# A hybrid trunk layer on one core: a written order that runs over both ends of the Strassen stage, layer norm in three steps, gate stores on SyncE

## The chip, the cores and the metric

The kernel runs on one core of one Trainium2 chip. The metric is the time of one execution on the device, in microseconds (us). A run's profile comes from one profiled execution; its span is the time from the first to the last instruction in the trace, and the execution's own time is a little longer.

The core's engines, as the profile names them: PE (TensorE, matmuls), PEld (its weight loads, which overlap PE), DVE (VectorE), ACT (ScalarE), POOL (GpSimd, here almost only an issuer of DMAs) and SP (SyncE, a queue of DMAs, "SPq" in the profile). Each engine works through its own list of instructions in order and waits on semaphores.

## The reference, cut to what matters

One layer, one batch, 1024 positions, 1024 channels, all in float32:

```python
h = rms_norm(x, g_mix)
z = h @ w_in + b_in                              # 1024 -> 7168 columns
va, ga, xb, gb, sa, sb = split(z, [1024, 1024, 1536, 1536, 1024, 1024])
u = causal_depthwise_conv(va * sigmoid(ga), conv_a_w, conv_a_b)     # width 31
y_a = silu(layer_norm(u, ln_g, ln_b)) @ w_a_out
v = causal_depthwise_conv(xb, conv_b_w, conv_b_b)                   # width 4
v = rg_lru(v, ...)                               # gates by 16 heads, linear recurrence
y_b = (v * gelu(gb)) @ w_b_out
m = sigmoid(sa) * y_a + sigmoid(sb) * y_b
x = x + m @ w_o
x = x + square(relu(rms_norm(x, g_mlp) @ w_1)) @ w_2
return rms_norm(x, g_final)
```

rg_lru computes a gate `a` and an input `b` for every position and channel and then the recurrence h[t] = a[t] h[t-1] + b[t].

## The kernel before, in words

Every matrix product is done in three matmuls: both operands are split into a high part (rounded to the format that TensorE reads at full rate) and a low part (the rest), and high x high, high x low and low x high are summed. A split is made in one of two ways. `split` (L51, L52): ACT copies the high part, DVE subtracts it from the source. `split_dma` (L65 to L67): ACT writes the negated high part into the low tile, a DMA issued by POOL adds the source to it in place (an accumulating DMA), and ACT copies the high part.

Activations are kept transposed: channels on the 128 partitions, positions along the row, in two halves of 512 (`HALVES`). A matmul is 128x128 by 128x512.

The stages, with their place in the profiled span:

- **Stage 1** (to about 369 us): the columns xb, va and ga of the in-projection, in 28 chunks of 128 columns (L686, 48 matmuls each). Beside it run, on ACT and DVE, the width-4 convolution (L437), the head gates (L485 to L493), the scans of the recurrence (`scan_tile`, L526 to L529, one for each of 12 tiles of channels; each result is stored to the DRAM tile `hd` on SP at L530), the product va * sigmoid(ga) (`u_out`, L540 and the DVE operation listed under L413), and the taps of the width-31 convolution (L579 to L595; each finished tile y0 to y7 is stored to `yd` and added to `ysum` at L602).
- **The z stage** (about 378 to 678 us): the columns gb, sa and sb. They are taken in 14 pairs of chunks; each pair is one 2x2 block product done by Strassen's scheme with 7 products (`z_mm`, L822, 12 matmuls each). So there are 98 steps, in the order `zseq`. For a product p, `z_sums` makes the weight sums on DVE, `z_lhs` splits the left operand (tile `zo`) by `split_dma`, `z_post` carries bank results from one product to the next, and `z_out` (L834 to L845) applies gelu or sigmoid. For gb the result is multiplied with the scan's tile, loaded back from `hd` by `z_h` (L853, tile `hb`), and stored to the DRAM tile `hgd`; for sa and sb it is stored to `gates`. Both stores are issued by POOL (L838, L845). The weights come by `z_load` (L779, tile `zw`) on SP. The right operand's sums (`xs` tiles) are made by `x_load`, `x_sum` (L630 and an accumulating DMA) and `x_parts`, from s = 22 of stage 1 (`XS`) into the z stage (`ZX`).
- **The out-projection b** (about 675 to 831 us): `hgd` is loaded as 12 tiles hg0 to hg11, each split, and eight tiles yb0 to yb7 are computed (L91, 72 matmuls each), each multiplied with a gate tile sb into m (L1008).
- **The layer norm** of the convolution's output runs beside yb: the mean `mu` by a matmul with a matrix of equal entries (L968), the eight tiles yn loaded and centred (L973), squared on ACT (L974) and summed on DVE (L976) into `vs`, the variance `var` by a second matmul (L980), the inverse root by `newton_rstd` (L96 to L104), then scaling (L985) and silu (L986). Then the tiles are split into suh and sul, and **ya0 to ya7** follow (L91, about 838 to 928 us).
- The o projection, the MLP up and down and the last norm take the rest, to 1649.7 us.

What sets the order: in stage 1 and the z stage the order is written out by hand (`tc.manual_schedule`), once for stage 1 and once for the z stage. Three clocks `clk` ("P", "A", "V" for PE, ACT and DVE) are advanced by planned costs (`at`), DVE's operations are put off by `later(ready, cost, f, ...)` and placed by `vector_work` in the order of their ready times; `fill(until)` puts convolution taps into DVE's free time as long as the next, at a planned 0.74 us, ends before `until`. After the z stage a scheduler orders the instructions, and the tile pools, whose tiles are reused in turn, set when a load can start: `T` (the large pool), `E` (a small pool of 7), and the z stage's own pools of 8 weight tiles, 4 sums and 7 evacuation tiles. The first tiles of the out-projection (`first_wb`, and the loop over hg0 to hg11) are given a high priority. A scan's step in the written order:

```python
if d == 0:
    scan_exp(g)
    scan_in(3 * g, 3 * g + 1)
elif d == 1:
    scan_in(3 * g + 2)
    scan_root(g)
else:
    for t in [3 * g + d - 2] if s < NC1 - 1 else range(3 * g + d - 2, 3 * g + 3):
        later(rooted[t], 4.8, scan_tile, t)
```

Here `s` is the chunk, `g` a group of three scans and `d` how many chunks have passed since the group's gates were ready.

Of the kernel before, what the change touches and what calls it, by code (L numbers as in the profile page):

```python
# [15 lines left out]
P = 128  # L16
# [14 lines left out]
def trunk_kernel(ctx: ExitStack, tc: tile.TileContext, x, xt_in, vecs, w_in, w_a_out, w_b_out,  # L31
# [358 lines left out]
    taps = {"wait": [], "now": None, "next": None, "left": 0}  # L390

    def fill(until):
        while clk["V"] + 0.74 <= until:
            if taps["now"] is None:
                if taps["next"] is None:
                    if not taps["wait"]:
                        return
                    taps["next"] = conv(taps["wait"].pop(0))
                    next(taps["next"])
                taps["now"], taps["next"], taps["left"] = taps["next"], None, 48  # L400
            if next(taps["now"], None) is None:
# [115 lines left out]
            nc.scalar.activation(r, r, AF.Sqrt)  # L517
            rooted[t] = at("A", 1.06)

    def scan_in(*ts):  # L520
        for t in ts:
            later(0, 1.27, nc.vector.tensor_tensor, gate[1, t], gate[1, t], vt.pop(t), ALU.mult)

    def scan_tile(t):
        a, r, i = at_.pop(t), gate.pop((0, t)), gate.pop((1, t))
# [27 lines left out]
    def conv(j):  # L553
        u = ut.pop(j)
        acc, tmp = T(f"y{j}"), T(f"yt{j}")
        xe, xo = (u[:, h] for h in HALVES)
        p0, p2 = (acc[:, h] for h in HALVES)
        xs, p1 = (tmp[:, h] for h in HALVES)
        bias = cab_c[:, j:j + 1]

        def tap(d):
            w = WA - 1 - d
            return caw[:, w * 8 + j:w * 8 + j + 1]

# [10 lines left out]
        def step(cost=0.74):  # L575
            at("V", cost)
            return True

        nc.vector.tensor_tensor(xs, xe, xo, add)  # L579
        yield step()  # L580
        nc.vector.tensor_scalar(p2, xs, tapsum(0), cab2[:, j:j + 1], ALU.mult, add)
        clk["V"] = max(clk["V"], begun)
        yield step(0.45)
        for k in range(1, NE):
            for o, a, c in ((p0, xe, tap(2 * k)), (p2, xs, tapsum(k)),
                            (p1, xo, tap(2 * k + 1) if k < NE - 1 else None)):
                if c is not None:
                    nc.vector.scalar_tensor_tensor(o[:, k:], a[:, 0:HS - k], c, o[:, k:],  # L588
                                                   ALU.mult, add)
                    yield step()  # L590
        nc.vector.tensor_tensor(p2, p2, p0, sub)
        yield step()
        nc.vector.tensor_tensor(p2, p2, p1, sub)
        yield step()
        nc.vector.tensor_tensor(p0[:, 1:], p0[:, 1:], p1[:, 0:HS - 1], add)  # L595
        nc.sync.dma_start(yd[j], acc)
        yield step()
        if j == 0:
            ysum.append(T("ysum"))
# [77 lines left out]
    def chunk_mm(s, n0, n1):  # L677
# [5 lines left out]
        for n in range(n0, n1):  # L683
# [9 lines left out]
    head_at = {s: n for n, s in enumerate(HS0)}  # L693

    EXP = {head_slot: g for g, head_slot in enumerate(HS0[4 * g + 3] + 1 for g in range(4))}
    XS = {22: ((x_load, 0),), 23: ((x_sum, 0, 11, 12),), 24: ((x_sum, 0, 22),),
          25: ((x_sum, 0, 21), (x_load, 1)), 26: ((x_parts, 0, 6, 7), (x_sum, 1, 11, 12)),
          27: ((x_sum, 1, 22), (x_parts, 0, 5, 4))}
    w_load(3)
    w_load(4)  # L700
    w_parts(3)
    with tc.manual_schedule(engines=ENGINES):
        for s in range(3, NC1):
# [32 lines left out]
            for d in range(5):  # L736
                if s - d in EXP:
                    g = EXP[s - d]
                    if d == 0:
                        scan_exp(g)  # L740
                        scan_in(3 * g, 3 * g + 1)
                    elif d == 1:
                        scan_in(3 * g + 2)
                        scan_root(g)
                    else:
                        for t in [3 * g + d - 2] if s < NC1 - 1 else range(3 * g + d - 2, 3 * g + 3):
                            later(rooted[t], 4.8, scan_tile, t)
            for f, *a in XS.get(s, ()):
                f(*a)
# [34 lines left out]
    def z_sums(i, p):  # L784

        def S_(n, a, b, op_):
            zs[i, n] = t = sp_.tile([P, HS], F32, tag="s", name=f"zs{n}_{i}").rearrange(
                "p (k c) -> p k c", c=P)
            later(0, 0.74, nc.vector.tensor_tensor, t, a, b, op_)

        if p == 7:
            S_(3, z_blk(i, 0, 0), z_blk(i, 1, 0), ALU.subtract)
        elif p == 6:
            S_(1, z_blk(i, 1, 0), z_blk(i, 1, 1), ALU.add)
            S_(2, zs[i, 1], z_blk(i, 0, 0), ALU.subtract)
        elif p == 5:
            S_(4, z_blk(i, 0, 1), zs[i, 2], ALU.subtract)

    def z_lhs(i, p):
        src = z_blk(i, *{1: (0, 0), 2: (0, 1), 4: (1, 1)}[p]) if p in (1, 2, 4) else \  # L800
            zs[i, {3: 4, 5: 1, 6: 2, 7: 3}[p]]
        o = wp.tile([P, 2, 4, P], F32R, tag="w", name=f"zo{i}_{p}")
        split_dma(src, o[:, 0], o[:, 1])
        at("A", 1.24)
        zo[i, p] = o

    def z_bank(i, b):
# [19 lines left out]
    def z_out(i, m_, hf, src, name):  # L827
# [3 lines left out]
        if ci < SA:  # L831
            t = ci - GB
            h = hb.pop((t, hf))
            nc.scalar.activation(a, src, AF.Gelu_apprx_tanh, bias=bias)  # L834

            def mult():
                nc.vector.tensor_tensor(h, h, a, ALU.mult)
                nc.gpsimd.dma_start(hgd[t, :, HALVES[hf]], h)  # L838

            later(at("A", 0.62), 0.74, mult)  # L840
# [14 lines left out]
    def z_post(i, p):  # L855
# [11 lines left out]
        elif p == 5:  # L867
            zb[i, "c"] = c = EV(f"zc22_{i}")
            nc.scalar.activation(c, zb[i, "e"], AF.Copy)
            later(at("A", 0.62), 0.74, nc.vector.tensor_tensor, c, c, zb[i, "f"], ALU.add)  # L870
        elif p == 3:
            z_out(i, 0, 1, zb[i, "e"], None)
        elif p == 4:
            c = zb[i, "u"]
            later(0, 0.74, nc.vector.tensor_tensor, c, c, zb[i, "f"], ALU.add)

    def z_post2(i, p):

# [8 lines left out]
    for i in range(2, NZ):  # L887
        zseq += [(i, 1), (i, 7), (i - 1, 3), (i, 6), (i, 2), (i - 1, 4), (i, 5)]
    zseq += [(NZ - 1, 3), (NZ - 1, 4)]
    ZX = {0: ((x_sum, 1, 21), (x_parts, 1, 6)), 1: ((x_parts, 1, 7),), 3: ((x_parts, 1, 5),),  # L890
          6: ((x_parts, 1, 4),)}
    H_AT = {2: (0, 0), 5: (1, 1), 3: (0, 1), 4: (1, 0)}
    loaded = 0
# [9 lines left out]
        return f(*zseq[n]) if 0 <= n < len(zseq) else None  # L903

    with tc.manual_schedule(engines=ENGINES):
        z_load_to(4)
        for n in range(4):
            z_get(n, z_sums)
# [30 lines left out]
    def E(name, dt=F32, shape=(P, S)):  # L939
        return ep.tile(list(shape), dt, tag="e", name=name)  # L940

    hg = []

    def first_wb():
        ws = []
        for n in range(2):
            raw = T(f"wb0_{n}")
            nc.sync.dma_start(raw[:, 0:6 * P].rearrange("p (k c) -> p k c", c=P), w_b_out[0, n])
            h = T(f"wb0h_{n}", F32R)
            l = T(f"wb0l_{n}", F32R)  # L950
            split(raw[:, 0:6 * P], h[:, 0:6 * P], l[:, 0:6 * P])
            ws += [(h[:, k * P:k * P + P], l[:, k * P:k * P + P]) for k in range(6)]
        return ws

    with tc.high_priority():
        wb0 = first_wb()
        for t in range(12):
            raw = T(f"hg{t}")
            nc.sync.dma_start(raw, hgd[t])
            h, l = (X1 if t == 0 else E if t < 2 else T)(f"hgh{t}", F32R), \  # L960
                (X1 if t == 0 else E if t < 3 else T)(f"hgl{t}", F32R)
            split(raw, h, l)
            hg.append((h, l))

    def layer_norm_steps():
        pm = PS("mu", "ps2")
        for hs in HALVES:
            nc.tensor.matmul(pm[:, hs], onesm, ysum[0][:, hs], start=True, stop=True)  # L968
        vs, sq = E("vs"), E("sq")
        for j in range(8):  # L970
            ya.append(T(f"yn{j}"))
            nc.sync.dma_start(ya[j], yd[j])
            nc.vector.tensor_tensor(ya[j], ya[j], pm, ALU.subtract)  # L973
            nc.scalar.activation(sq if j else vs, ya[j], AF.Square)  # L974
            if j:
                nc.vector.tensor_tensor(vs, vs, sq, ALU.add)  # L976
        yield
        pv = PS("var", "ps2")
        for hs in HALVES:
# [21 lines left out]
    for j in range(8):  # L1001
# [677 lines left out]
```

## Time and profile before

| | us |
| --- | --- |
| median of 3 runs | 1652.23 (1651.26 to 1656.23) |
| the profiled execution's own time | 1651.43 |
| its span | 1649.7 |
| PE busy | 1581.7 (96%) |
| DVE busy | 1096.1 (66%) |
| ACT busy | 875.5 (53%) |
| POOL busy | 235.5 (14%) |

The mean granted clock of TensorE was 0.984 of full speed. The DMA queues moved 308.58 MB. How to read the views: the rows of busy tenths cut the span into 40 slices and give the busy share of each in tenths; the views of waits name an engine, the line that waited, and whose event ended the wait; a timeline lists single instructions with start and duration, and in brackets the idle time before them; the windows give busy times and, at the end, the granted clock, the DMA share and the rate in GB/s. E means the end of the z stage's last product where the text says so.

### The profile page before, as it was taken

Reading aid. Unit: us, or ns where it says so; the run is one execution under the profiler, and the core shown is the slowest. Engines: PE = TensorE matmul, PEld = TensorE weight load, DVE = VectorE, ACT = ScalarE, POOL = GpSimd, SP = SyncE. Lnnn points to the kernel's source line nnn. Section 1 sums busy time; section 2 is a strip of 40 time slices with the busy share of each in tenths; the row PEclk is TensorE's granted clock in tenths of the full one; section 3 lists DMA queues with packets and bytes.
Section 4 is the critical chain, followed back from the end, with each engine's and each line's share of the span. In section 5 each row is a group of like instructions: output and inputs, shape, how many; then the busy total and the mean of one; then the engine's idle time right before and its main releaser. Section 6 shows DMA issues by size and latency. Waiting matters only on the chain.

```text
span 1649.7 us, 18943 instructions
## 1 busy us (share of the span) xinstructions
PE 1581.7 (96%) x6910; PEld 1289.5 (78%) x6910; DVE 1096.1 (66%) x1456; ACT 875.5 (53%) x1168; POOL 235.5 (14%) x306
## 2 busy tenths in 40 slices
PE   8999999995999999799989999999999999999998
PEld 6878888774778887588768888788888888888886
DVE  6688798883555776773853235875555457888888
ACT  5548577565657666422373315654444456555552
POOL 0000000113344443200121100000000001111110
PEclk9999999997999999899999999999999999999999
DMA  9567887999899889836576542433333578988852
GB/s 364 150 169 180 215 217 191 257 216 231 209 261 243 223 210 238 259 87 171 171 212 189 117 147 90 156 138 115 108 110 104 174 246 215 229 208 215 216 129 102
DMA packets 102317, 308.58 MB, mean 187 GB/s; under 512 B 11936, under 2 KB 13472, under 8 KB 102224
## 3 DMA queue, kind: packets, MB, share of 16 engines
q1 hardware_dynamic: 62832, 193.36, 35.5%
q0 software_dynamic: 39248, 113.76, 32.5%
q8 instruction: 54, 0.88, 0.2%
q14 instruction: 39, 0.32, 0.1%
q10 hardware_dynamic: 144, 0.26, 0.0%
HBM read 146.11 MB, written 54.53 MB: 122 GB/s over the span
## 4 chain that ended last, share of the span: by engine, by line
PE 74%; issue 9%; DMA 9%; DVE 4%; ACT 2%; POOL 1%; POOLq 0%; SPq 0%; ACTq 0%; DVEq 0%
PE z L686 14%; PE d L1462 14%; PE ya L91 5%; PE o L1061 3%; DMA zo<-zw 2%; PE e L1577 2%; PE keep L1462 2%; DMA zo<-zs 2%; PE o L91 2%; PE z L257 2%; PE rg L485 1%; PE rg L487 1%; PE rg L486 1%; POOL zo L66 1%; PE o L1085 1%
## 5 line engine op out<-in xcount | busy, mean ns | idle before, releaser
L686 PE MATMUL z<-xh,win_h 128*128 128x512 f32 x400 | 123.4, 390 | 0.0
L686 PE MATMUL z<-xl,win_h 128*128 128x512 f32 x400 | 123.2, 389 | 0.0
L1474 DVE TENSOR_TENSOR acc<-acc,d 128x1024 f32<-128x1024 f32 x72 | 87.8, 1220 | 33.3 <-PE d L1462 32.7
L686 PE MATMUL z<-xh,win_l 128*128 128x512 f32 x400 | 98.1, 391 | 0.0
L588 DVE SCALAR_TENSOR_TENSOR y<-u,vec,y 128x511 f32<-128x511 f32 (+14 forms) x120 | 88.4, 737 | 0.0
L686 PEld LDWEIGHTS z<-xh,win_l 128*128 128x128 f32 x400 | 75.1, 188 | 16.9
L686 PEld LDWEIGHTS z<-xh,win_h 128*128 128x128 f32 x400 | 75.1, 188 | 16.2
L686 PEld LDWEIGHTS z<-xl,win_h 128*128 128x128 f32 x400 | 75.1, 188 | 15.8
L493 ACT ACTIVATE g<-rg,vec 96x1024 f32<-96x1024 f32 x32 | 35.7, 1114 | 96.7 <-PE rg L487 58.6
L588 DVE SCALAR_TENSOR_TENSOR y<-yt,csum,y 128x511 f32<-128x511 f32 (+6 forms) x112 | 82.6, 737 | 0.0
L588 DVE SCALAR_TENSOR_TENSOR yt<-u,vec,yt 128x511 f32<-128x511 f32 (+6 forms) x112 | 82.6, 737 | 0.0
L66 POOL DMA_DIRECT2D win_l<-win_raw x25 | 21.7, 870 | 280.2 <-ACT win_l L65 228.8
L66 POOL DMA_DIRECT2D zo<-zs x56 | 50.2, 906 | 75.4 <-ACT zo L65 73.8
L437 DVE SCALAR_TENSOR_TENSOR v<-xb,vec,v 128x1023 f32<-128x1023 f32 (+2 forms) x36 | 46.2, 1282 | 19.6 <-ACT v L428 18.9
L1255 ACT ACTIVATE fa<-fa 128x512 f32<-128x512 f32 x16 | 10.1, 631 | 89.9 <-DVE fa L1233 89.9
L1195 ACT ACTIVATE o<-s 128x512 fp32r<-128x512 f32 x64 | 38.1, 622 | 29.5 <-DVE s L1187 26.1
L66 POOL DMA_DIRECT2D db_1l<-wr x7 | 6.1, 870 | 328.7 <-DMA wr<-in_w_dram 265.0
L65 ACT ACTIVATE zo<-zs 128x512 fp32r<-128x512 f32 x56 | 35.0, 626 | 29.6 <-issue 15.6
L91 PE MATMUL ya<-suh,wa_h 128*128 128x512 f32 x128 | 40.3, 398 | 7.8 <-ACT suh L51 7.8
L1109 DVE TENSOR_TENSOR o<-w_raw,o 128x512 fp32r<-128x512 f32 x40 | 27.5, 689 | 29.2 <-ACT o L1195 29.2
L1109 DVE TENSOR_TENSOR o<-s,o 128x512 fp32r<-128x512 f32 x64 | 42.5, 686 | 4.7 <-ACT o L1195 4.6
L66 POOL DMA_DIRECT2D zo<-zw x42 | 36.5, 868 | 59.1 <-ACT zo L65 54.1
(1595 smaller groups left out, 4620.6 us busy)
## 6 DMA issues: line engine op xcount, KB each, us to landing
fr<-fd SPq DMA_DIRECT2D x32, 512.0 KB, 5.2
wr<-in_w_dram SPq DMA_DIRECT2D x32, 512.0 KB, 6.2
w_raw<-in_w_dram SPq DMA_DIRECT2D x31, 512.0 KB, 4.4
zw<-in_w_in_dram SPq DMA_DIRECT2D x28, 512.0 KB, 5.6
zo<-zs POOLq DMA_DIRECT2D x56, 256.0 KB, 4.9
win_raw<-in_w_in_dram SPq DMA_DIRECT2D x25, 512.0 KB, 6.7
win_l<-win_raw POOLq DMA_DIRECT2D x25, 512.0 KB, 5.6
zo<-zw POOLq DMA_DIRECT2D x42, 256.0 KB, 4.0
```

The costliest lines, as they stand in the source:

```text
L65: nc.scalar.activation(l, src, AF.Copy, scale=-1.0)
L66: nc.gpsimd.dma_start(l, src, accum_op=ALU.add)
L91: nc.tensor.matmul(ps[:, HALVES[hf]], a, b[hf], start=i == 0, stop=i == len(todo) - 1)
L437: nc.vector.scalar_tensor_tensor(v[:, d:S], a[:, 0:S - d], cbw_c[:, w * 12 + t:w * 12 + t + 1], v[:, d:S], ALU.mult, ALU.add)
L493: nc.scalar.activation(a, gps.pop((n, gi))[:HD, :], AF.Sigmoid, bias=(ba_c, bx_c)[gi][:, n:n + 1])
L588: nc.vector.scalar_tensor_tensor(o[:, k:], a[:, 0:HS - k], c, o[:, k:], ALU.mult, add)
L686: nc.tensor.matmul(zps[s][:, HALVES[hf]], w[:, k, :], xw[k][part][hf], start=n == 0, stop=n == 23)
L1061: nc.tensor.matmul(ps[:, HALVES[hf]], tok(a, k, t), wo[k][b][:, HALVES[hf]], start=k == 0 and b == 0 and n == 0, stop=k == 7 and b == 1)
L1109: tt(l, src, h.bitcast(F32), ALU.subtract)
L1195: nc.scalar.activation(o[:, 0], src, AF.Copy)
L1462: nc.tensor.matmul(o, a, b, start=n == 0 and (p != 1 or g == 0), stop=n == len(todo) - 1, skip_group_check=p == 1 and g > 0)
L1474: tt(acc[p, q2], acc[p, q2], ps, ALU.add)
```

## The change

Five things are edited.

1. Planned costs: a tap 0.67 for 0.74, a sum or short DVE operation 0.63 for 0.74, a scan's input product 1.2 for 1.27.
2. Stage 1: the scans' input products get a ready time; a scan's place by `d` is written anew, so that the last group's three scans come closer together; the `xs` sums start one chunk earlier.
3. z stage: the seventh product's left operand is split by ACT and DVE, not by DMA; the `hgd` and `gates` stores are issued by SP.
4. The loads and splits of wb0 and of hg0 to hg11 are put into the written order, inside the z stage's last 14 steps and the steps behind it. Raw wb0 tiles come from the z stage's weight pool, the split tiles from `T` (and one from `X1`).
5. The layer norm has three steps for two: the yn loads; mu, centring and squares with two `sq` tiles; variance and the rest. The steps are taken after yb2, yb3 and yb4, and taps are filled without limit from yb2 on.

```diff
-        while clk["V"] + 0.74 <= until:
+        while clk["V"] + 0.67 <= until:
...
-    def scan_in(*ts):
+    def scan_in(ready, *ts):
         for t in ts:
-            later(0, 1.27, nc.vector.tensor_tensor, gate[1, t], gate[1, t], vt.pop(t), ALU.mult)
+            later(ready, 1.2, nc.vector.tensor_tensor, gate[1, t], gate[1, t], vt.pop(t), ALU.mult)
...
-    XS = {22: ((x_load, 0),), 23: ((x_sum, 0, 11, 12),), 24: ((x_sum, 0, 22),),
-          25: ((x_sum, 0, 21), (x_load, 1)), 26: ((x_parts, 0, 6, 7), (x_sum, 1, 11, 12)),
-          27: ((x_sum, 1, 22), (x_parts, 0, 5, 4))}
+    XS = {22: ((x_load, 0),), 23: ((x_sum, 0, 11, 12),), 24: ((x_sum, 0, 22), (x_load, 1)),
+          25: ((x_sum, 0, 21), (x_sum, 1, 11, 12)), 26: ((x_parts, 0, 6, 7), (x_sum, 1, 22)),
+          27: ((x_parts, 0, 5, 4), (x_sum, 1, 21))}
...
                     if d == 0:
                         scan_exp(g)
-                        scan_in(3 * g, 3 * g + 1)
+                        scan_in(begun + 3.5, 3 * g, 3 * g + 1)
                     elif d == 1:
-                        scan_in(3 * g + 2)
+                        scan_in(begun + 3.5, 3 * g + 2)
                         scan_root(g)
-                    else:
-                        for t in [3 * g + d - 2] if s < NC1 - 1 else range(3 * g + d - 2, 3 * g + 3):
+
+                    for t in range(3 * g, 3 * g + 3):
+                        if d == (t - 3 * g + 2 if g < 3 else 1 + (t - 3 * g) // 2):
                             later(rooted[t], 4.8, scan_tile, t)
...
-        split_dma(src, o[:, 0], o[:, 1])
-        at("A", 1.24)
+        if p == 7:
+            nc.scalar.activation(o[:, 0], src, AF.Copy)
+            later(at("A", 0.6), 0.63, nc.vector.tensor_tensor, o[:, 1], src, o[:, 0].bitcast(F32),
+                  ALU.subtract)
+        else:
+            split_dma(src, o[:, 0], o[:, 1])
+            at("A", 1.15)
...
-                nc.gpsimd.dma_start(hgd[t, :, HALVES[hf]], h)
+                nc.sync.dma_start(hgd[t, :, HALVES[hf]], h)
...
-            nc.gpsimd.dma_start(spill[b, j, :, HALVES[hf]], a)
+            nc.sync.dma_start(spill[b, j, :, HALVES[hf]], a)
...
-    ZX = {0: ((x_sum, 1, 21), (x_parts, 1, 6)), 1: ((x_parts, 1, 7),), 3: ((x_parts, 1, 5),),
+    ZX = {0: ((x_parts, 1, 6),), 1: ((x_parts, 1, 7),), 3: ((x_parts, 1, 5),),
...
+        L = len(zseq)
+        ZX.update({L - 14: ((wb0_load, 0),), L - 13: ((wb0_load, 1),), L - 11: ((wb0_parts, 0),),
+                   L - 10: ((wb0_parts, 1), (hg_load, 0)), L - 9: ((hg_load, 1),),
+                   L - 8: ((hg_parts, 0), (hg_load, 2)), L - 7: ((hg_parts, 1), (hg_load, 3)),
+                   L - 6: ((hg_parts, 2, 3), (hg_load, 4)), L - 5: ((hg_parts, 4), (hg_load, 5, 6)),
+                   L - 4: ((hg_parts, 5, 6), (hg_load, 7)), L - 3: ((hg_load, 8),),
+                   L - 2: ((hg_parts, 7, 8), (hg_load, 9)), L: ((hg_load, 10), (hg_parts, 9)),
+                   L + 1: ((hg_load, 11), (hg_parts, 10, 11))})
...
     def layer_norm_steps():
+        for j in range(8):
+            ya.append(T(f"yn{j}"))
+            nc.sync.dma_start(ya[j], yd[j])
+        yield
...
-        vs, sq = E("vs"), E("sq")
+        vs, sqs = E("vs"), [E("sq0"), E("sq1")]
         for j in range(8):
-            ya.append(T(f"yn{j}"))
-            nc.sync.dma_start(ya[j], yd[j])
+            sq = sqs[j % 2] if j else vs
             nc.vector.tensor_tensor(ya[j], ya[j], pm, ALU.subtract)
-            nc.scalar.activation(sq if j else vs, ya[j], AF.Square)
-            if j:
-                nc.vector.tensor_tensor(vs, vs, sq, ALU.add)
+            nc.scalar.activation(sq, ya[j], AF.Square)
+            if j > 1:
+                nc.vector.tensor_tensor(vs, vs, sqs[(j - 1) % 2], ALU.add)
+        nc.vector.tensor_tensor(vs, vs, sq, ALU.add)
...
-        fill(clk["V"] + 13.5 if j < 4 else math.inf)
-        if j in (4, 5):
+        fill(clk["V"] + (10, 14)[j] if j < 2 else math.inf)
+        if j in (2, 3, 4):
             next(ln_it, None)
```

`hg_load` issues the load of an hg tile on SP, `hg_parts` splits it (ACT copies the high part, DVE subtracts); `wb0_load` and `wb0_parts` do the same for the two halves of yb0's weights. They take the place of `first_wb` and of the loop over hg0 to hg11.

More of the change, by code (lines that the diff above doesn't have):

```diff
@@ L573, in conv, with step @@
         yield True
[L575 removed]
+        def step(cost=0.67):
             at("V", cost)
@@ L788, in S_ @@
                 "p (k c) -> p k c", c=P)
-            later(0, 0.74, nc.vector.tensor_tensor, t, a, b, op_)
+            later(0, 0.63, nc.vector.tensor_tensor, t, a, b, op_)
         if p == 7:
@@ L837, in mult @@
                 nc.vector.tensor_tensor(h, h, a, ALU.mult)
-                nc.gpsimd.dma_start(hgd[t, :, HALVES[hf]], h)
-            later(at("A", 0.62), 0.74, mult)
+                nc.sync.dma_start(hgd[t, :, HALVES[hf]], h)
+            later(at("A", 0.62), 0.63, mult)
         else:
@@ L869, in z_post @@
             nc.scalar.activation(c, zb[i, "e"], AF.Copy)
-            later(at("A", 0.62), 0.74, nc.vector.tensor_tensor, c, c, zb[i, "f"], ALU.add)
+            later(at("A", 0.62), 0.63, nc.vector.tensor_tensor, c, c, zb[i, "f"], ALU.add)
         elif p == 3:
@@ L874, in z_post @@
             c = zb[i, "u"]
-            later(0, 0.74, nc.vector.tensor_tensor, c, c, zb[i, "f"], ALU.add)
+            later(0, 0.63, nc.vector.tensor_tensor, c, c, zb[i, "f"], ALU.add)
     def z_post2(i, p):
@@ L905, in trunk_kernel, with wb0_load, wb0_parts, hg_load @@
     with tc.manual_schedule(engines=ENGINES):
+        hg, hraw, wb0, wb0_ = [], {}, [], []
+        def wb0_load(n):
+            wb0_.append(wp.tile([P, 8, P], F32, tag="w", name=f"wb0_{n}"))
+            nc.sync.dma_start(wb0_[n][:, 0:6, :], w_b_out[0, n])
+        def wb0_parts(n):
+            h, l = ((T)(f"wb0{x}_{n}", F32R)[:, 0:6 * P].rearrange("p (k c) -> p k c", c=P) for x in "hl")
+            raw = wb0_[n][:, 0:6, :]
+            nc.scalar.activation(h, raw, AF.Copy)
+            later(at("A", 0.8), 0.9, nc.vector.tensor_tensor, l, raw, h.bitcast(F32), ALU.subtract)
+            wb0.extend((h[:, k, :], l[:, k, :]) for k in range(6))
+        def hg_load(*ts):
+            for t in ts:
+                hraw[t] = T(f"hg{t}")
+                nc.sync.dma_start(hraw[t], hgd[t])
+        def hg_parts(*ts):
+            for t in ts:
+                h, l = ((T if t else X1)(f"hg{x}{t}", F32R) for x in "hl")
+                raw = hraw.pop(t)
+                nc.scalar.activation(h, raw, AF.Copy)
+                later(at("A", 1.0), 1.2, nc.vector.tensor_tensor, l, raw, h.bitcast(F32), ALU.subtract)
+                hg.append((h, l))
+        L = len(zseq)
[6 more added lines that the diff above has]
+                   L + 1: ((hg_load, 11), (hg_parts, 10, 11))})
         z_load_to(4)
@@ L940, in E @@
         return ep.tile(list(shape), dt, tag="e", name=name)
[L942 to L963, printed above, removed]
     def layer_norm_steps():
+        for j in range(8):
+            ya.append(T(f"yn{j}"))
+            nc.sync.dma_start(ya[j], yd[j])
+        yield
         pm = PS("mu", "ps2")
```

## The prediction, as put on record

> **What bounds the kernel now.** I read first the rows of busy tenths (40 slices of 41.2 us), to see where TensorE (PE) is not full.
>
> ```profile
> PE   8999999995999999799989999999999999999998
> ...
> PEclk9999999997999999899999999999999999999999
> ...
> DMA  9567887999899889836576542433333578988852
> ```
>
> PE is 96% busy over the span; between the first slice and the last it falls under 9 only in the 10th (371 to 412 us), the 17th (660 to 701) and the 21st (825 to 866). The granted clock dips in the first two, and DMA is near full there. Then the waits of PE, which name what ended each stop (total, times, longest):
>
> ```profile
> PE z0a L822 <- DMA zo<-zw: 11.5, 1, 11.5
> PE z0a L822 <- ACT zo L67: 8.2, 1, 8.2
> PE ya L91 <- ACT suh L51: 7.8, 1, 7.8
> ...
> PE yb L91 <- ACT hgh L51: 4.0, 2, 3.7
> PE var L980 <- DVE vs L976: 3.1, 1, 3.1
> PE yb L91 <- ACT wb1a_h L67: 3.0, 1, 3.0
> PE z1b L822 <- DMA zo<-zs: 2.0, 1, 2.0
> PE z13a L822 <- DMA zo<-zw: 1.9, 1, 1.9
> ```
>
> Then PE's timeline around the first stop, and SyncE's queue there:
>
> ```profile
> 365.77 3.79 PE L686 MATMUL z<-xh,win_l 128*128 128x512 f32 x16
> 377.72 0.80 PE L822 MATMUL z0a<-xh,zo 128*128 128x512 f32 x1 [8.16 <-ACT zo L67]
> 378.31 0.63 PE L822 MATMUL z0a<-xl,zo 128*128 128x512 f32 x1
> 390.43 1.22 PE L822 MATMUL z0a<-xh,zo 128*128 128x512 f32 x2 [11.48 <-DMA zo<-zw]
> ```
> ```profile
> 364.82 6.22 SPq L530 DMA_DIRECT2D hd<-g  x2
> 371.08 2.54 SPq L779 DMA_DIRECT2D zw<-in_w_in_dram  x4
> ```
>
> Sixteen matmuls in 3.79 us, the last taking 0.39, give the pitch: (3.79 - 0.39) / 15 = 0.227 us. Whatever start-to-start time exceeds 0.227 per matmul is lost; that counts a stop and the slow matmuls behind it. Summed (leaving out excesses under 0.3): **joint 1** (365 to 394) 21.9 us; **opening of the z stage** (415 to 534) 6.5; **its tail** (635 to 672) 6.5; **joint 2** (678 to 702) 12.3; **layer norm** 17.6 (mu 0.8, var 7.0, ya0 9.8). Together 64.8 us, 3.9% of the time. All that the change can gain is here; no matmul is removed. The SyncE rows show joint 1's cause: the zw loads stand behind two hd stores that wait for the scans.
>
> Last the windows (span, then busy us and count of PE, PEld, DVE, ACT, POOL, the clock, DMA share, GB/s):
>
> ```profile
> 365.00:400.00 35.00, 15.36 (x56) 11.64 (x55) 12.54 (x14) 16.35 (x24) 8.12 (x10) 0.71 0.99 237
> 440.00:480.00 40.00, 38.40 (x167) 30.83 (x167) 23.12 (x35) 25.77 (x46) 16.33 (x22) 1.00 1.00 259
> 640.00:680.00 40.00, 34.48 (x147) 27.09 (x146) 28.73 (x41) 26.53 (x43) 13.74 (x19) 1.00 0.91 256
> 680.00:700.00 20.00, 13.95 (x43) 9.69 (x44) 13.76 (x18) 7.18 (x9) 4.04 (x7) 0.80 0.78 249
> ```
>
> DVE, ACT and POOL have room in every row; DMA has almost none at 365, 440 and 640.
>
> **The change part by part.** All is summed against the profiled execution: 1651.4 us (span 1649.7), 0.8 below the median of 1652.2.
>
> *Joint 1.* One scan is 1.21 + 1.23 + 2.29, about 4.7 us. The last three now run from 350.4 to 370.7 with taps and u6 (1.26) between them. In the new order they stand together, ahead of u6: from about 349 they end near 349 + 3 x 4.7 = 363, so the last hd store and the zw loads behind it issue near 363 instead of 371.1. Now zw lands 5.4 us after issue and PE starts 1.2 later (376.5, 377.7); that would be 368.5, before PE's last matmul of stage 1 ends (369.5). But the change also puts xs21_1 ahead of the first zo split on ACT, and it waits for the accumulate of xs22_1. In the old order xs22_1 itself came at 370.0, after 8.2 us of waiting; in the new it comes about a chunk (48 matmuls, 10.9 us) earlier, and its accumulate and xs21_1 follow. I take ACT free at 371 to 372, PE's start at 373.5: the stop shrinks from 8.3 to 4.0. The second stop is the accumulate of zo's low half by DMA, 12.9 us from its issue at 377.44; the 42 of that kind have a median of 4.0. With DMA still full and xs21_1's accumulate ahead of it on POOL I take 7: ready at 380, a stop of 5.5 instead of 11.9. Slow matmuls 1.5. New loss 11.0, **gain 10.9**; ends: 2 (low half as late as now) and 18 (4.0 each).
>
> *z stage.* The seventh product is split by ACT and DVE: 14 DMAs of 256 KB and 14 ACT operations go, 14 DVE subtractions of 0.69 us come, 9.7 us on a DVE that is 50 to 73% busy. 24 hgd stores and 32 gates stores leave POOL (0.58 to 0.82 us each there) for SyncE. Bytes change only by the 14 accumulates, out of 98: one seventh of that traffic. Waits on zo make up all of the opening's 6.5 us and most of the tail's; I take 2.5 of the opening back (ends -3 and 5.5). In the tail the 12 hg loads (6.3 MB, 25 us at 250 GB/s) and the wb0 pair come earlier into a window whose DMA share is already 0.91, while stores no longer stand ahead of accumulates on POOL; I take 2.0 back (ends -6, all waits doubled, and 6). The lower planned costs (0.67 for a tap, measured 0.65 to 0.66 apart; 0.63 for a sum) only pack more taps into DVE's idle time.
>
> By the Trainium skill ("DMA: Bandwidth & Descriptors", section "Issuing engines are not separate DMA queues"), DMAs issued by ScalarE, SyncE or GpSimd run on the same 16 engines, and spreading them saves only issue time. The trace agrees so far (share 1.00 at 440 to 480, with POOL busy 16.3 of 40): by it the moved stores give nothing, and the tail's 2.0 falls out of the sum.
>
> *Joint 2.* Now yb stops 3.2 for wb1a_h and 3.8 for an hgh that waits for its load; 5.3 are slow matmuls and small stops. In the new order wb0 and hg0 to hg8 are split before the last product ends (call that E), and yb0 opens with 40 matmuls (9.1 us) on hg0 to hg9. Left: hg11. Its load stands behind the store of conv y6, which ends about E+6, and two raw wb2 loads; it lands 6.4 us after issue (median), so hgh11 is ready at E+13 to E+17; PE wants it 67 matmuls in, at E+15.2. I take 3 for that and 1 for hgl9: new loss 4, **gain 8.3** (ends 3 and 12).
>
> *Layer norm.* mu moves up one yb tile (16.3 us), so y7 must be summed by E+65.3. DVE starts y7 behind m0, which waits for yb0's last matmul, 96 in (E+21.8); y7 and its sum took 717.7 to 753.2 = 35.5, so E+58.5: cover 7 us, and what joint 2 loses moves both. yn loads come before mu, so the 6.6 us in which DVE waited for yn go. From mu to var DVE has 8 subtractions, 7 additions and m4, 16 x 1.17 + 1.9 = 20.6 us; PE has 86 matmuls, 19.5. So var still waits about 1.5. Then the root, the reciprocal (6.55) and the scaling took 802 to 829.5 and silu to 837.7; from var at E+86.5 that ends near E+116, and yb7 ends at E+132. Only suh2 to suh7 are left on ACT behind wa1's split; the order gives each at 0.96 us against 1.13 us of matmuls. New loss 3.5 (0.5, 2, 1), **gain 14.1** (ends 6 and 16.5).
>
> By the Trainium skill ("TensorE: Matmul & The Clock Gate", section "What's actually happening") the clock falls after an idle window of about 3.4 us. The trace differs: var's wait of 3.08 is followed by 3.8 us of excess, while the waits of 1.6 to 1.9 at 637 to 663 stand in windows of clock 1.00. By the rule var would give 3.8 less.
>
> *Added waits.* SyncE issues in order, and a store now holds it until ACT or DVE has made the tile; behind it stand the zw and hb loads. Cover, from pair 7: its zw loads issue at 508.5, z7a's first matmul is at 530.3; 21.8 less landing 5.6, a split 1.2 and an accumulate 4.0 leaves 11 us. I charge 2 us in all (ends 0 and the slower rival below).
>
> Sum: 10.9 + 2.5 + 2.0 + 8.3 + 14.1 - 2 = 35.8 us; 1651.4 - 35.8 = 1615.6, on the median's footing 1616.4.
>
> **The rivals.** *Transfers are hidden behind nothing: DMA is the limit.* Share 0.99 at joint 1 and 0.91 in the tail speak for it: earlier issues then land no earlier, and only the stall for wb1a_h, some of joint 1's first stop and the layer norm (which needs ACT and DVE) come back: 4 + 3 + 14 = 21, less 2: 1633. Against it: between 687 and 698 the DMA view shows 309 to 422 GB/s, so 237 at joint 1 is not a ceiling of bytes.
>
> *SyncE becomes the bound: slower.* Place: each of the 14 z pairs. Four stores of 4.2 us (issue to landing) in the way of the zw loads, each issued only when an earlier place in the queue has landed, would be 16.8 us; it decides once the loads come over 11 us late. Then 12 pairs stop 5.8 us each: 70, less the 36: 1687. For it: SyncE now already waits 92 us on zo accumulates before zw loads. Against: the stores follow PE's own pace and most stand behind the loads.
>
> *The change doesn't do what it says:* ACT's hgh splits, standing ahead of zo's and the z copies in the last pair, wait for hg loads held up on SyncE, and what joint 2 gains the tail gives back, while xs21_1 does the same at joint 1. With layer norm pushed late by y7 (cover 7 us) little is left: 1648.
>
> *Nearly all comes back:* accumulates at 4.0 us, hg11 in time: 1651 - 52 = 1600.
>
> **How the numbers follow.** Forecast 1616 (its own range 1604 to 1628): 0.58. DMA limit, 1633: 0.18. Nearly all, 1600: 0.10. No gain, 1648: 0.06. SyncE, 1687: 0.08. A change of 0.3% (5 us) is about what a measurement of this kernel can tell from none. Faster by more: 0.58 + 0.18 + 0.10 = 0.86; within: 0.06; slower: 0.08. The range takes in the first three: 1597 to 1641.
>
> **What would show it.** Right: zw issued near 363; z0a's two stops near 4 and 5.5; no wait of yb on wb1a_h; var's under 2, ya0's under 1.5. Wrong: SyncE rows with long waits on ACT or DVE ahead of zw loads, new PE waits on zo inside the z stage, or a wait of mu on ysum.

## The result, and the profile after

| | before | after |
| --- | --- | --- |
| median of 3 runs, us | 1652.23 | 1629.3 (1629.29 to 1630.67) |
| profiled execution, us | 1651.43 | 1630.67 |
| span, us | 1649.7 | 1628.5 |
| PE busy, us | 1581.7 | 1571.9 |

The ratio of the times is 0.9858, 95% interval 0.9832 to 0.9884: 22.9 us faster, where 35.8 were forecast. The direction is right and the time lies in the stated range (1597 to 1641), but 1.3 us outside the forecast's own (1604 to 1628), and two of the terms, joint 1 and the z stage's tail, came out with the other sign. The interval is 4 us to either side, so differences of under 5 us between the runs below are read from PE's stops and not from the times alone.

The rows of busy tenths of the changed kernel, the same ones as in the prediction:

```profile
PE   8999999995999999889999999999999999999997
...
PEclk9999999997999999999999999999999999999999
...
DMA  9566887997899888937585642533333569888852
```

The 21st slice (layer norm) is full now and the clock's second dip is gone, but the 10th slice still stands at 5 with the clock at 7. The waits of PE say the same (total, times, longest; rows of other stages left out):

```profile
PE z0a L828 <- DMA zo<-zw: 9.9, 1, 9.9
PE z0a L828 <- ACT zo L67: 9.4, 1, 9.4
...
PE yb L91 <- ACT hgh L935: 5.1, 2, 4.8
PE z L686 <- DMA win_l<-win_raw: 1.9, 1, 1.9
PE z13e L828 <- ACT zc L875: 1.7, 1, 1.7
PE z13a L828 <- DMA zo<-zw: 1.5, 1, 1.5
...
PE var L1002 <- DVE vs L998: 0.4, 1, 0.4
```

The two waits at joint 1 were 11.5 and 8.2 before and are 9.9 and 9.4 now. The wait of yb for wb1a_h is gone, that for an hgh has grown from 3.7 to 4.8; ya0's 7.8 is gone and var's fell from 3.1 to 0.4. PE's lost time by place, summed as in the prediction (start-to-start time over 0.227 us per matmul, excesses under 0.3 left out):

| us lost at | before | forecast | after |
| --- | --- | --- | --- |
| joint 1 | 21.9 | 11.0 | 23.7 |
| opening of the z stage | 6.5 | 4.0 | 4.7 |
| its tail | 6.5 | 4.5 | 7.3 |
| joint 2 | 12.3 | 4.0 | 7.6 |
| layer norm | 17.6 | 3.5 | 2.3 |

These sum to 64.8 and 45.6: 19.2 of the 20.8 us between the two profiled executions. So the layer norm gave three quarters of the gain (15.3), joint 2 gave 4.7, the opening 1.8; the tail lost 0.8 more, and joint 1, where 10.9 were forecast, lost 1.8 more. The table rests on one profile of each kernel.

Joint 1 in the changed kernel: SyncE's queue, then the first zo split on ACT with what stands ahead of it, then PE.

```profile
355.32 9.97 SPq L530 DMA_DIRECT2D hd<-g  x3
365.39 5.04 SPq L780 DMA_DIRECT2D zw<-in_w_in_dram  x4
```
```profile
378.64 1.06 ACT L630 ACTIVATE xs<-xs 128x1024 f32<-128x1024 f32 x1 [7.58 <-DMA xs<-xu]
379.60 0.61 ACT L65 ACTIVATE zo<-zw 128x512 fp32r<-128x512 f32 x1
```
```profile
367.51 3.92 PE L686 MATMUL z<-xh,win_l 128*128 128x512 f32 x16 [1.86 <-DMA win_l<-win_raw]
380.79 0.79 PE L828 MATMUL z0a<-xh,zo 128*128 128x512 f32 x1 [9.36 <-ACT zo L67]
381.38 0.63 PE L828 MATMUL z0a<-xl,zo 128*128 128x512 f32 x1
391.88 1.22 PE L828 MATMUL z0a<-xh,zo 128*128 128x512 f32 x2 [9.87 <-DMA zo<-zw]
```

The scans did what the edit says: zw is issued 5.7 us earlier (365.39 against 371.08). Yet PE starts 3.1 us later than before (380.79 against 377.72). And stage 1's own last weights now come late: 1.86 us for win_l.

### The profile page after: what moved, and what is told of

It reads as the page before. It is cut to its first block, busy times and chain, and to the rows that moved or that the text cites. A ratio compares the mean times of both kernels' runs of the same rounds, so it can differ in the third digit from the quotient of the medians.

```text
span 1628.5 us, 18931 instructions
## 1 busy us (share of the span) xinstructions
PE 1571.9 (97%) x6910; PEld 1284.6 (79%) x6910; DVE 1105.8 (68%) x1470; ACT 867.9 (53%) x1154; POOL 191.8 (12%) x236
## 4 chain that ended last, share of the span: by engine, by line
PE 78%; DMA 8%; issue 8%; DVE 3%; ACT 2%; POOL 1%; SPq 0%; POOLq 0%; ACTq 0%; DVEq 0%
PE z L686 14%; PE d L1484 14%; PE ya L91 5%; PE yb L91 3%; PE o L1083 3%; PE e L1599 2%; PE keep L1484 2%; PE o L91 2%; DMA zo<-zw 2%; PE z L257 2%; DMA zo<-zs 2%; PE rg L485 1%; PE rg L487 1%; PE rg L486 1%; PE o L1107 1%
## 5 line engine op out<-in xcount | busy, mean ns | idle before, releaser
L66 POOL DMA_DIRECT2D zo<-zs x42 | 36.7, 874 | 140.8 <-ACT zo L65 133.8
L1115 DVE TENSOR_TENSOR x<-xr,o 128x1024 f32<-128x1024 f32 x8 | 9.6, 1219 | 52.2 <-PE o L1083 37.7
L1046 DVE TENSOR_TENSOR sa<-ya,sa 128x1024 f32<-128x1024 f32 x8 | 9.8, 1226 | 46.4 <-PE ya L91 46.4
```

The lines of the kernel that those rows point to most:

```text
L66: nc.gpsimd.dma_start(l, src, accum_op=ALU.add)
```

## The experiments

Two theories of joint 1. **Q**: ACT's queue; the first split waits behind xs21_1, as the rows above suggest. **D**: the 16 DMA engines are full from about 355 to 395 us, most of their time with accumulating DMAs, and whatever is asked for earlier lands when the backlog is through. Beside them SyncE's order at joint 2, the worth of the moved stores and of the seventh product, and the layer norm by itself.

**xs21_1 behind the first zo splits again** (Q against D):

```diff
-          27: ((x_parts, 0, 5, 4), (x_sum, 1, 21))}
+          27: ((x_parts, 0, 5, 4),)}
...
-    ZX = {0: ((x_parts, 1, 6),), 1:
+    ZX = {0: ((x_sum, 1, 21), (x_parts, 1, 6)), 1:
```

> The changed kernel with one thing undone: the sum xs21_1 is made behind the first zo splits again, as before the change. In the changed kernel PE's first stop at joint 1 is 9.4 us (ended by ACT's first zo split, which came right behind xs21_1, for which ACT had waited 7.6 us) and the second 9.9 us (the accumulate of zo's low half). Theory Q (ACT's queue: the split waits behind xs21_1): the first stop falls to 3 to 5 us and the loss at joint 1 from 23.7 to 16 to 19 us; 1622 to 1625 us. Rival D (the 16 DMA engines are full from 355 to 395 us, so zw and the accumulates land when the backlog is through, whatever order they are asked for): zw itself lands only at 377 or later, the first stop stays at 8 or more or what it loses the second gains; loss at joint 1 22 to 24 us, 1627 to 1630 us.

Measured: 1629.8 us (ratio to before 0.9862, 0.9847 to 0.9876). ACT's first zo split in this run:

```profile
379.24 0.63 ACT L65 ACTIVATE zo<-zw 128x512 fp32r<-128x512 f32 x1 [7.48 <-DMA zw<-in_w_in_dram]
```

The split is free of xs21_1, and starts within 0.4 us of where it did, because zw itself lands only now, 13.2 us after its issue at 366.05. The first stop is 10.3 us. The second fell to 7.1; that zo's accumulate no longer follows that of xs21_1 on POOL fits this, but is not tested by itself. Joint 1 lost 19.9, less than D expected and more than Q; the time did not follow (joint 2 lost 2.7 more). **Q falls as the main cause of the first stop.** It is not nothing: in the changed kernel the trace has the first zw load landing at 377.64, 12.2 us after its issue, so there xs21_1 held the split for the last 2.0 us (to 379.60). The row "<-DMA xs<-xu" names the wait that came last, and behind it stood one nearly as long.

All runs together say the same of D. In the nine kernels that keep the four xs accumulates of the first half (the kernel before and the changed one among them) the first zw load was issued between 365.4 and 372.6 us and landed between 375.9 and 379.2; the earliest issues are not the earliest landings.

**The first three zo tiles split by ACT and DVE:**

```diff
-        if p == 7:
+        if p == 7 or (i, p) in ((0, 1), (1, 1), (0, 2)):
             nc.scalar.activation(o[:, 0], src, AF.Copy)
```

> The changed kernel with the first three zo tiles split by ACT and DVE and not by an accumulating DMA. DVE is idle from 373 to 388 us in the changed kernel. If the second stop at joint 1 (9.9 us) is the accumulate in a full DMA queue (theory D), it falls under 2 us, with the first stop still near 9 us behind xs21_1 (theory Q): loss at joint 1 near 14 us, 1619 to 1622 us. Rival: the backlog only moves, since the other loads and accumulates are still there, and the z stage's opening waits for the next zo or xs tiles instead: 1625 to 1629 us with new waits between 392 and 420 us.

Measured: 1622.6 us (0.9818, 0.9803 to 0.9833). PE's waits from 362 to 400 us in this run:

```profile
PE z0a L828 <- ACT zo L805: 9.3, 1, 9.3
PE z1a L828 <- ACT zo L805: 1.7, 1, 1.7
```

z0a's second stop is gone, the first (9.3) is not; joint 1 lost 14.7, the opening 5.7. The time is 0.6 us above the expected 1619 to 1622, nearer to the theory than to the rival.

**The four first xs parts split by ACT and DVE** (four accumulating DMAs of 512 KB fewer, in front of zw):

```diff
-            if c2 == 0:
+            if c2 == 2:
                 split_dma(src, h, l)
```

> The changed kernel with the four xs parts of the first half of positions (xs6, xs7, xs5, xs4) split by ACT and DVE, so that four accumulating DMAs of 512 KB are gone between 358 and 385 us; zo's first splits are as in the changed kernel. Theory D (accumulates fill the 16 engines: 4.8 MB of POOL's DMAs take 72% of their time from 360 to 395 us, 4.2 MB of SyncE's 32%): zw lands 5 to 8 us after its issue and not 13 to 16; the first stop falls from 9.4 to 1 to 4 us and the second from 9.9 to 4 to 7; 1615 to 1621 us. Rival (zw's landing is set by the loads themselves or by what DVE delays: the scans' stores): first stop still 7 or more, 1626 to 1630 us.

Measured: 1621.4 us (0.982, 0.9798 to 0.9842). ACT's first zo split and PE's two stops:

```profile
372.12 0.63 ACT L65 ACTIVATE zo<-zw 128x512 fp32r<-128x512 f32 x1 [1.46 <-DMA zw<-in_w_in_dram]
```
```profile
373.32 0.50 PE L828 MATMUL z0a<-xh,zo 128*128 128x512 f32 x1 [2.94 <-ACT zo L67]
...
381.80 1.22 PE L828 MATMUL z0a<-xh,zo 128*128 128x512 f32 x2 [7.75 <-DMA zo<-zw]
```

zw is issued at the same time (365.11) and lands 7.0 us later, not 12.2. The first stop fell to 2.9, as D said, the second only to 7.75, where 4 to 7 were expected: the low half is still an accumulate. Joint 1 lost 13.5. D's mechanism in numbers is the DMA view from 360 to 395 us (packets, MB, time taken as a share of 16 engines), first the changed kernel, then this run:

```profile
q0 software_dynamic: 1683, 5.10, 74.6%
q1 hardware_dynamic: 1258, 4.04, 31.1%
```
```profile
q0 software_dynamic: 1251, 3.22, 49.5%
q1 hardware_dynamic: 1244, 3.98, 29.9%
```

q0 carries POOL's DMAs, here all accumulates; q1 SyncE's plain ones. 74.6% of 35 us for 5.10 MB is 5.1 us a MB, 31.1% for 4.04 MB is 2.7: a byte that is accumulated costs 1.9 times a plain one. (The shares are packet times; the two add to 106%, so the figures are rough. The second pair gives 5.4 and 2.6.) By these figures, as an estimate, 16 full engines move some 370 GB/s of plain bytes and 195 of accumulated ones, so 237 GB/s at joint 1 before the change was a full queue.

That POOL issues them is not what costs. In the kernel before, from 687 to 698 us, POOL's queue carried mostly plain loads (the gate tiles sb):

```profile
q0 software_dynamic: 604, 2.13, 52.7%
q1 hardware_dynamic: 574, 1.83, 41.1%
```

Here a MB of q0 took 2.7 us and one of q1 2.5. No run has plain copies from tile to tile, as most of the accumulates are, so the part that this has in the 1.9 stays open.

**Stage 1 as before** (scans, ready times, xs sums), the rest as changed:

> The changed kernel with its stage 1 edits undone: the scans' places, their ready times and the xs sums as before; the z stage, the stores, joint 2 and the layer norm as changed. The changed kernel loses 23.7 us at joint 1, before it lost 21.9. Theory: the stage 1 edits gave nothing, and without them the loss at joint 1 is 21 to 23 us again: 1627 to 1629.5 us. Rival: they help the z stage's opening or the taps (y6, y7) and so the layer norm: 1631 to 1635 us.

Measured: 1629.3 us (0.9859, 0.9845 to 0.9874), joint 1 lost 24.6, the opening 3.2. As the theory had it: in the changed kernel the whole of the stage 1 edits is worth nothing that can be measured. zw is issued at 372.60 here, 7.2 us later than in the changed kernel, and lands at 377.23, 0.4 us earlier.

**hg11's load one step earlier:**

```diff
-L: ((hg_load, 10), (hg_parts, 9)),
+L: ((hg_load, 10), (hg_parts, 9), (hg_load, 11)),
-                   L + 1: ((hg_load, 11), (hg_parts, 10, 11))})
+                   L + 1: ((hg_parts, 10, 11),)})
```

> The changed kernel with the load of hg11 written one step earlier, right behind hg10's, so that it no longer stands behind the y6 store, the two raw wb2 loads and a gates store on SyncE. In the changed kernel it is issued at 691.2 us and PE stops 4.85 us for hgh11 at 697. Theory (SyncE's order): the stop falls under 1 us and the loss at joint 2 from 7.6 to 2 to 3 us: 1624 to 1626.5 us. Rival (DMA is full here, 0.85 of the share at 680 to 700 us): the load lands later than 6 us after its issue and the stop stays at 3 or more: 1627 to 1629 us.

SyncE's queue in the changed kernel, then in this run:

```profile
682.76 0.32 SPq L596 DMA_DIRECT2D yd<-y  x1
687.91 0.33 SPq L60 DMA_DIRECT2D wb2a_raw<-in_w_b_out_dram  x1
690.39 0.33 SPq L60 DMA_DIRECT2D wb2b_raw<-in_w_b_out_dram  x1
690.82 0.38 SPq L851 DMA_DIRECT2D gates<-zu  x1
691.25 0.42 SPq L929 DMA_DIRECT2D hg<-hgd  x1
```
```profile
673.90 0.89 SPq L929 DMA_DIRECT2D hg<-hgd  x2
682.52 0.33 SPq L60 DMA_DIRECT2D wb2a_raw<-in_w_b_out_dram  x1
```

Measured: 1625.2 us (0.9841, 0.982 to 0.9863; its runs spread from 1620.4 to 1629.0). Joint 2 lost 0.5 instead of 7.6. The theory holds at the stop: the load was late by SyncE's order. In the time, 4.1 us lie within the spread, and the profiled execution is the fastest of the four. In the changed kernel the last hg row is issued 14.8 us after the one before it (676.48), behind four DMAs whose tiles or results it does not need. What SyncE waited for there, from 680 to 700 us:

```profile
SPq L596 <- DVE y L595: 5.8, 1, 5.8
SPq L60 <- DMA wb1a_l<-wb1a_raw: 4.4, 1, 4.4
SPq L60 <- DMA wb1b_l<-wb1b_raw: 2.0, 1, 2.0
```

**The stores back on POOL:**

```diff
-                nc.sync.dma_start(hgd[t, :, HALVES[hf]], h)
+                nc.gpsimd.dma_start(hgd[t, :, HALVES[hf]], h)
...
-            nc.sync.dma_start(spill[b, j, :, HALVES[hf]], a)
+            nc.gpsimd.dma_start(spill[b, j, :, HALVES[hf]], a)
```

> The changed kernel with the hgd and gates stores issued by POOL again, as before the change. Theory: with the same bytes on the same 16 engines the issuing queue matters little; 1628 to 1631 us, z stage's loss (opening and tail, 12.0 us in the changed kernel, 13.0 before) 11 to 14 us. Rival A (stores on POOL stand ahead of accumulates there): z stage's loss rises by 3 or more, 1632 to 1636 us. Rival B (stores on SyncE hold up zw and hg loads): the loss falls by 3 or more and joint 2's too, 1622 to 1627 us.

Measured: 1624.5 us (0.9846, 0.9821 to 0.987; its runs spread from 1622.6 to 1630.3). The z stage lost 10.9 (12.0 in the changed kernel), joint 2 nothing: without these stores in front, all hg loads are out by 671 us. This is rival B in time and at joint 2, where the move to SyncE was a loss; the z stage's fall is smaller than it expected. By the Trainium skill ("DMA: Bandwidth & Descriptors", section "Issuing engines are not separate DMA queues") DMAs from several engines run on the same 16 DMA engines, and issuing them on several saves only the issue time. The z stage of this pair agrees (1.1 us apart), and joint 2 shows what else the choice decides: which loads stand behind a store that waits for its data.

**The seventh product by DMA again** (`if p == 8` in place of `if p == 7`):

> The changed kernel with the seventh product's left operand split by an accumulating DMA again (14 DMAs more, 14 DVE subtractions fewer). Theory (in the z stage the accumulates keep DMA full): the z stage's loss rises from 12 to 15 to 19 us and the time to 1632 to 1637 us. Rival (DMA has room outside the two joints, share 0.80 to 0.84 from 520 to 640 us): within 2 us, 1628 to 1631 us.

Measured: 1634.5 us (0.9898, 0.9879 to 0.9918). The opening lost 7.7 and the tail 8.3, 16.0 against 12.0. The theory: 14 accumulates are worth about 5 us (1634.5 against 1629.3).

**The layer norm's part alone, on the kernel before:**

> The kernel before with the layer norm's part alone: yn loads in a step of their own, two squares' tiles, the steps after yb2, yb3 and yb4, and the taps filled without limit from yb2 on; nothing else. Theory: the layer norm's gain (17.6 us lost before, 2.3 in the changed kernel) needs nothing of the other parts: loss there 2 to 5 us, 1636 to 1640 us. Rival (y7 is later here, since y6 ends 24 us after the z stage and not 6, so mu waits for ysum): mu stops 5 to 15 us and the time is 1642 to 1650 us.

Measured: 1636.9 us (0.9919, 0.9898 to 0.994). Layer norm lost 1.7, joint 1 22.0, joint 2 12.0. As the theory had it; 14 to 16 us of the change's 22.9 (14.3 by the medians of this run, 15.9 by the stops) come from this part, and it needs none of the others.

**Together:** both splits by ACT and DVE, xs21_1 behind, hg11 early.

> The changed kernel with four edits of earlier runs together: the first three zo tiles and the four first xs parts split by ACT and DVE, xs21_1 behind the first zo splits, hg11's load behind hg10's. Theory D (the accumulating DMAs were the bound at joint 1, SyncE's order that of joint 2): the effects add, since they lie in different stops: joint 1 loses 4 to 7 us and not 23.7, joint 2 under 2 and not 7.6, 1604 to 1608 us. Rival (the two edits at joint 1 took the same backlog away, and the opening of the z stage then waits for its own zo or xs tiles): joint 1 loses 9 or more or the opening 9 or more, 1611 to 1616 us.

Measured: 1606.4 us (0.9734, 0.9712 to 0.9756). Joint 1 lost 4.5, joint 2 1.3, opening 6.5, tail 6.0. The effects at joint 1 add, as D has it: the splits of zo alone took 9.0 off its 23.7, those of xs alone 10.2, and both (with xs21_1 behind) 19.2; the opening lost 1.8 more than in the changed kernel. PE at joint 1:

```profile
372.20 0.67 PE L828 MATMUL z0a<-xh,zo 128*128 128x512 f32 x1 [2.40 <-ACT zo L805]
372.66 0.63 PE L828 MATMUL z0a<-xl,zo 128*128 128x512 f32 x1
373.09 1.05 PE L828 MATMUL z0a<-xh,zo 128*128 128x512 f32 x2
```

**The same, with the stores on POOL and hg11 in its late place:**

> As the run before it, but hg11's load stays in its late place and the hgd and gates stores go back to POOL. If at joint 2 the stores on SyncE were the thing in front of hg11 (theory), both cures are worth the same: within 2 us of the run before it, 1604 to 1609 us, joint 2 under 2 us. Rival (POOL's accumulates in the z stage now wait behind stores): the opening and the tail together lose 3 us more than there, 1608 to 1612 us.

Measured: 1610.2 us (0.9745, 0.9726 to 0.9764). Joint 2 lost nothing, but the opening and the tail 18.0, against 12.5: the rival, with single stops of 4.2 us (z8a) and 4.1 (z12e). In the other pair of kernels that differ in the stores the z stage went the other way (10.9 on POOL, 12.0 on SyncE). What the stores' queue is worth inside the z stage stays open.

**Three more zo tiles by ACT and DVE, at the tail** ((12, 5), (13, 2), (13, 4) added to the list):

> As the first run of this set, with three more zo tiles split by ACT and DVE, those of products 5 of pair 12 and 2 and 4 of pair 13, where PE still waits for accumulates at the z stage's tail. Theory (DMA is full there, 0.97 at 640 to 680 us, and a tile that needs no accumulate is not late): the tail loses 1 to 2.5 us and not 4 to 5, 2 to 3 us under the first run. Rival (DVE, 82% busy there, is late instead, or the taps that give way push y6 and y7 out): no faster, tail or layer norm lose 4 or more.

Measured: 1604.6 us (0.9714, 0.9694 to 0.9735). The tail lost 3.3 instead of 6.0, DVE is busy 38.15 of 40 us there, and layer norm lost 3.0 against 3.3. The tail stays above the 1 to 2.5 us expected, and the 1.8 us in time are less than the two intervals can tell apart. Nor is the tail's gain clear by itself: in kernels whose edits lie elsewhere the tail lost from 3.8 (xs parts by DVE) to 8.6 us (stage 1 as before). It is the fastest kernel of the study by its median. (Its first stop at joint 1 was 5.0 us and not 2.4: the scans and zw's issue, at 368.09, came 3.8 us later, which no edit explains.)

**Together, with the scans in the old order:**

> The kernel with the four edits together (zo and xs split by ACT and DVE, xs21_1 behind, hg11 early), with the scans' order of the kernel before: taps and u6 between the last three scans again. Theory: with DMA no longer full, zw lands 5 to 7 us after its issue, so the issue now sets PE's start, and the old order (zw issued 6 to 8 us later) costs what it could not cost before: joint 1's first stop grows from 2.4 to 7 to 10 us, 1611 to 1615 us. Rival (the scans' order is worth nothing here either): within 2 us of 1606.4.

Measured: 1618.6 us (0.9807, 0.9776 to 0.9838). SyncE's queue, first with the new order, then with the old:

```profile
364.34 4.46 SPq L780 DMA_DIRECT2D zw<-in_w_in_dram  x4
```
```profile
378.92 2.16 SPq L779 DMA_DIRECT2D zw<-in_w_in_dram  x4
```

PE's first stop in the old order:

```profile
384.61 0.80 PE L827 MATMUL z0a<-xh,zo 128*128 128x512 f32 x1 [14.53 <-ACT zo L804]
```

zw lands 5.0 us after issue here, and PE's first stop is 14.5 us. The stage 1 edits, the new order among them, were worth nothing behind the backlog; without it the order is worth 12 us. This is more than expected: two of the xs subtractions and a wait of 3.6 us now also stand ahead of the last two scans on DVE, so the 12 us are the price of the old order with these splits, not of the order alone.

## Why the prediction was right, and where it was wrong

**The total.** It lies in the range because the range takes in the rivals. The forecast's own mechanism gave 1616.4; 1629.3 is 12.9 us from that and 3.7 from the rival "DMA is the limit". What carried the gain is the layer norm, which was sized rightly; the largest error is joint 1.

**The bound.** Right: no matmul was removed, and the places that lost time were the ones named. 19.2 of 20.8 us were regained there.

**Joint 1 (10.9 forecast, -1.8 measured): the failed step.** The issue time was right to 2.4 us (363 forecast, 365.4). Wrong was what followed: "that would be 368.5", an issue plus the 5.4 us that the load took before. zw took 12.2 us, and the accumulate of zo's low half, taken at 7, took 11.2 (380.60 to 391.83). The stops forecast at 4.0 and 5.5 came as 9.4 and 9.9, and the accumulate of stage 1's last weights, in the same queue, added 2.0. In the kernel before, zw was issued when a backlog had nearly landed: ACT had got its xs tile at 370.0, one accumulate and two stores were still under way at 371.1, and the DMA view shows 389 to 431 GB/s from 373 to 376. In the changed one four accumulates and two stores were under way at its issue (those of win_l, xs6, xs7 and xs22_1, issued on POOL from 356.8 to 365.0). Of the runs that took accumulates away, one removed the second stop and the other most of the first, and the order of xs21_1, which the prediction did weigh, was worth 2.0 us. "237 at joint 1 is not a ceiling of bytes" was an error of reading: the engines were full (share 0.99), and the bytes were few because accumulated ones cost 1.9 times as much. The rival "DMA is the limit" was the right mechanism for this term, at 0.18 instead of most of the weight; its time, 1633, was 4 us off: the 4 it gave joint 2 and the 14 of the layer norm came as 4.7 and 15.3, its 3 at joint 1 as -1.8.

**z stage (2.5 and 2.0 forecast; 1.8 and -0.8).** The opening is near, and the run with the seventh product by DMA shows the reason (4 us of the z stage's stops, 3.0 of them in the opening). The tail's 2.0 did not come. The share from 640 to 680 us rose from 0.91 to 0.97, as the end that was named has it (more traffic in a full window); but the tail differs by up to 4.8 us among kernels that leave it alone, so one profile shows neither the sign of this term nor its cause.

**Joint 2 (8.3 forecast, 4.7 measured).** The mechanism was the one written down, hg11 behind the y6 store and two raw wb2 loads. The term was mis-sized: a ready time of E+13 to E+17 was taken; the z stage ended at 676.5 us, and hgh11 was split at 697.0, 20.5 us after it. The y6 store in front waited 5.8 us for DVE, the wb2 loads 4.4 and 2.0 for the accumulates of wb1's tiles (until 687.9 and 690.4), and a gates store stood there too.

**Layer norm (14.1 forecast, 15.3 measured).** Right in the steps that were forecast: mu did not wait for ysum, var waited 0.4 (1.5 forecast), ya0 not at all. The part alone on the kernel before shows that it needs no other.

**The added waits on SyncE (2 us).** SyncE's waits ahead of the stores, from 400 to 680 us:

```profile
SPq L844 <- DVE hb L843: 105.0, 24, 31.0
SPq L851 <- ACT ze L849: 61.9, 15, 7.5
SPq L851 <- ACT zc L849: 21.3, 7, 3.4
SPq L851 <- ACT zu L849: 14.8, 7, 5.7
```

So SyncE waits 105 us for DVE's hb tiles and 98 for ACT's gates, but neither ACT nor DVE has a wait for a zw load from 400 to 680 us: the cover held, and the slower rival did not occur. (Its sum, 1651.4 + 70 - 36, gives 1685 and not 1687; nothing hangs on that.) The loss came at joint 2.

**"No gain" and "nearly all".** Neither. 1600 would have needed the accumulates at 4.0 us; the kernels that need fewer of them, and load hg11 in time, came near it (1606.4 and 1604.6).

## What to carry to other kernels

Before moving a load earlier, look at what is under way in front of it at its new place. A full DMA share alone does not tell: zw landed 5.4, 7.0 and 12.2 us after its issue in stretches whose share was 0.99 or more. Where several accumulating DMAs stand in front, an earlier issue bought no earlier landing here, and the thing to remove is that traffic, for which an idle DVE can stand in. On an in-order queue ask of every load what the DMAs in front of it wait for. When an edit moves nothing, it may be hidden behind another limit: test it again once that limit is gone.

## What the runs showed of the hardware

- An accumulating DMA took 1.9 times as much of the DMA engines' time per byte as a plain load or store (5.1 against 2.7 us a MB of all 16 engines, 360 to 395 us of the changed kernel), while plain loads on POOL's queue took 2.7 against 2.5 on SyncE's (687 to 698 us of the kernel before).
- At a full DMA share the first zw load, 512 KB, landed 12.2 us after its issue with four accumulates and two stores under way (changed kernel, 270 GB/s over that stretch), and 5.4 with one accumulate and two stores (kernel before, 330 GB/s).
- The stop of 2.4 us in the kernel with both splits is followed by matmuls 0.43 us apart (372.66 to 373.09); the granted clock there was 0.59 from 372 to 374 us, 0.55 from 374 to 376, and 1.00 before and after. By the Trainium skill ("TensorE: Matmul & The Clock Gate", section "What's actually happening") it takes an idle window of about 3.4 us; here a stop of 2.4, with one of 0.9 six us ahead of it, was enough.
